# The first norm of token blocks 1 to 3 from a second layout of x

## The chip, the cores and the metric

The kernel runs on one core of a Trainium2 chip. The metric is device time of one execution in microseconds. Three runs of the kernel before took 2847.90, 2848.84 and 2848.22 us: median 2848.22. PE is TensorE, PEld its weight loads, DVE VectorE, ACT ScalarE, POOL GpSimd, and SP the engine whose queue starts every DMA here.

## The reference

One layer of a transformer trunk over 2048 tokens of 1024 features. Only the part at the start of it is touched:

```python
h = modulate(rms_norm(x, norm_g[i, 0]), sh_m, sc_m)   # h * (1 + scale) + shift
y = stick_breaking_mixer(h, sb_w_qkv[r], sb_w_o[r])   # 16 heads, first step h @ w_qkv
x = x + gt_m * rms_norm(y, norm_g[i, 1])
h = modulate(rms_norm(x, norm_g[i, 2]), sh_f, sc_f)
y = swiglu_ffn(h, ffn_w_in[i], ffn_w_out[i])
x = x + gt_f * rms_norm(y, norm_g[i, 3])
```

`rms_norm` divides each token's features by the root of their mean square and multiplies by a gain for each feature; `modulate` has a scale and a shift for each feature. So the first `h` is `x[t, d] * rstd[t] * g_eff[d] + shift[d]`: one number for a token, two for a feature.

## The kernel before, in words

The tokens are worked in four blocks of 512 (`BT`), the 1024 features in eight chunks of 128 (`KC`). Matrix products want `h` with features on the partitions, and they run as three float32r products (`mm3`, lines 169 to 171) of a high and a low part: high is the value rounded to float32r, low is the value less high. So a chunk of `h` is two 128x512 tiles, `hl[:, 0]` and `hl[:, 1]`, kept in pairs of chunks as `ht` tiles.

The projections make queries, keys and values for two heads at a time (a pair `p`) and one token block `b`. `STEPS` lists them: (0, 0), (1, 0), (0, 1), (0, 2), (0, 3), then the other pairs. A step (`project`) is a generator with three products of eight slices each: keys (t = 1), queries (t = 0), values (t = 2); a slice is one `mm3`, three 128x512 matmuls. The first 42 slices after step (0, 0) run by themselves; after that `project_to` mixes slices with the stages of attention (score, two sigmoids on ACT, a scan on DVE, a product on POOL, transposes on PE, their split into high and low on ACT and DVE, the weighing of values on PE). The four compute engines work in the order in which this code issues, each its own queue from front to back; the order of SP's transfers is the scheduler's.

The first norm of block `b` is issued from inside the step before it and its own first product:

- `x_load(b)`: four loads of 128 tokens, in tiles named `x`, from SP (line 306). Block 1 is loaded during step (0, 0); blocks 2 and 3 in the first slice of the keys product before.
- `x_square(b, i)`, slices 0 to 3 of the queries product: the sum of squares on ACT (line 160), its mean on DVE (162), the power -1/2 on POOL (164).
- `x_scale(b, i)`, slices 4 to 7: `xn` = x times the token's number, on DVE (315).
- `first_norm(b, k)`: chunks 0, 1 and 2 in slices 2, 4 and 6 of the values product, chunk k + 3 in slice k of the block's own keys product. `x_turn` transposes the chunk for four groups of 128 tokens on PE (324) into one PSUM tile `xT`; `modulate` makes `hf` = xT * gain + shift on ACT (334), the high part by a cast on DVE (340) and the low part by a subtraction (342), on DVE for blocks 1 and 2 and on POOL for block 3 (`HOW`). After two chunks SP stores the pair in `h_s` for the other heads (363).

The keys product of a step reads chunk k in slice k, so PE waits there for a chunk that isn't done. Block 0 goes another way (`full_high`, `low`), which the edit leaves.

Tiles come from pools by a tag with a fixed number of buffers: `v` 7 (the `x` tiles, values), `kt` 7 (`xn`, keys), `ht` 5, `tmp` 4 (`hf`). In PSUM, `tps` has two banks and `accps` three, which also hold the products' sums.

Of the kernel before, what the change touches and what calls it, by code (L numbers as in the profile page):

```python
# [9 lines left out]
F32 = mybir.dt.float32  # L10
# [64 lines left out]
HOW = ["aav", "avv", "avv", "avp"]  # L75


def f32(ap):
    return ap.bitcast(F32)
# [22 lines left out]
def hybrid_trunk_kernel(  # L102
    ctx: ExitStack,
    tc: tile.TileContext,
    x: bass.AP,
    c: bass.AP,
# [193 lines left out]
    x_tiles, x_norm, x_rstd = {}, {}, {}  # L300

    def x_load(b):
        for i in range(4):
            r0 = b * BT + i * P
            xt = att.tile([P, D], F32, name=f"x{b}_{i}", tag="v", bufs=BUFS["v"])
            nc.sync.dma_start(xt, x[r0 : r0 + P])
            x_tiles[b, i] = xt

    def x_square(b, i):
        xn = att.tile([P, D], F32, name=f"xn{b}_{i}", tag="kt", bufs=BUFS["kt"])  # L310
        x_norm[b, i] = xn
        x_rstd[b, i] = rms_scale(att, x_tiles[b, i], f"n0_{b}_{i}", junk=xn)
# [5 lines left out]

    def x_turn(b, k):

        pool, tag = (tps, "t") if b < 2 else (accps, "acc")
        pt = pool.tile([P, BT], F32, name=f"xT{b}_{k}", tag=tag)
        for i in range(4):
            nc.tensor.transpose(
                pt[:, i * P : (i + 1) * P], x_norm[b, i][:, k * P : (k + 1) * P], ident
            )
        return pt

    def modulate(hl, pt, which, k, name, how="aap"):

        full = att.tile([P, BT], F32, name=name, tag="tmp", bufs=BUFS["tmp"])
        gain, add = g_eff[:, which, k : k + 1], shift[:, which, k : k + 1]
        if how[0] == "a":
            nc.scalar.activation(full, pt, AF.Identity, bias=add, scale=gain)
        else:
            nc.vector.tensor_scalar(full, pt, gain, add, op0=ALU.mult, op1=ALU.add)
        if how[1] == "a":
            nc.scalar.copy(hl[:, 0], full)
        else:
            nc.vector.tensor_copy(hl[:, 0], full)  # L340
        eng = nc.gpsimd if how[2] == "p" else nc.vector
        eng.tensor_tensor(hl[:, 1], full, f32(hl[:, 0]), op=ALU.subtract)
# [11 lines left out]
    def first_norm(b, k):  # L354
# [6 lines left out]
        modulate(norm_h[b][k], x_turn(b, k), 0, k, f"hf{b}_{k}", HOW[b])  # L361
# [23 lines left out]
    def project(at):  # L385
# [10 lines left out]
        def product(t):  # L396
# [8 lines left out]
            for k in range(KC):  # L405
# [11 lines left out]
                if t == 0 and nb:  # L417
                    (x_square if k < 4 else x_scale)(nb, k % 4)
# [1187 lines left out]
```

## Time and profile before

| | us |
|---|---|
| median of three runs | 2848.22 |
| profiled execution | 2849.01 |
| its span, first to last instruction | 2846.9 |
| PE busy | 2797.7 |
| PE weight loads busy | 2333.6 |
| DVE busy | 2031.8 |
| ACT busy | 1629.6 |
| POOL busy | 1278.3 |

The granted clock of TensorE is 1.0 throughout. A row of the timeline has the start in us from the span's start, the duration, the engine, the line of the kernel, the operation, the tiles written and read, the shapes and the count; in brackets stands the idle time of the engine before it and what ended it. Matmuls are pipelined: each lasts longer than the time to the start of the next, so PE's pace is read from starts. A group's row has the count, then the busy time in us and the mean in ns, then the idle time before. All the first norm lies before 150 us.

### The profile page before, as it was taken

How to read it: one execution, taken by the hardware profiler on the slowest of the kernel's cores; microseconds unless marked ns; L12 is line 12 of the kernel's file. 1: busy time of each engine (PE TensorE's matmuls, PEld its weight loads, DVE VectorE, ACT ScalarE, POOL GpSimd, SP SyncE). 2: the span in 40 equal slices, each digit the busy share in tenths (PEclk: the TensorE clock that was granted, in tenths of full speed). 3: DMA queues.
4: the chain of work that ended last, by engine and by line, in shares of the span. 5: the costliest groups of instructions: out<-in, count | busy, mean ns of one | idle time of the engine just before them, and what ended most of it. 6: DMA issues, size and time to landing. Idle time of an engine off the chain costs nothing.

```text
span 2846.9 us, 41792 instructions
## 1 busy us (share of the span) xinstructions
PE 2797.7 (98%) x13848; PEld 2333.6 (82%) x13848; DVE 2031.8 (71%) x2825; ACT 1629.6 (57%) x3263; POOL 1278.3 (45%) x2032
## 2 busy tenths in 40 slices
PE   7999999999999999999999999999999999999998
PEld 6788888888888888887888888888788888888887
DVE  6788898888888888888866766555775665133477
ACT  4787877788787877777645533333433333322343
POOL 1475666666576655656410122221222222544454
PEclk9999999999999999999999999999999999999999
DMA  8765546656665635546289645334463335545565
GB/s 323 276 210 168 189 153 229 211 173 231 189 208 192 207 119 179 196 132 231 88 300 310 205 137 152 122 97 162 130 176 109 112 107 163 191 142 155 180 215 193
DMA packets 239368, 516.84 MB, mean 182 GB/s; under 512 B 22320, under 2 KB 110384, under 8 KB 221488
## 3 DMA queue, kind: packets, MB, share of 16 engines
q1 hardware_dynamic: 239152, 514.18, 55.7%
q8 instruction: 109, 1.79, 0.3%
q14 instruction: 107, 0.88, 0.1%
HBM read 346.85 MB, written 118.49 MB: 163 GB/s over the span
## 4 chain that ended last, share of the span: by engine, by line
PE 88%; DVE 5%; issue 2%; ACT 2%; DMA 1%; POOL 1%; SPq 0%; DVEq 0%; POOLq 0%; ACTq 0%
PE s L169 9%; PE s L171 9%; PE s L170 9%; PE z L528 8%; PE o L607 8%; PE t L579 8%; PE pj L169 6%; PE pj L170 6%; PE pj L171 6%; PE o L171 5%; PE o L169 5%; PE o L170 5%; PE y L171 1%; PE y L169 1%; PE y L170 1%
## 5 line engine op out<-in xcount | busy, mean ns | idle before, releaser
L569 POOL TENSOR_TENSOR a<-a,w 128x512 f32<-128x512 f32 (+3 forms) x640 | 620.0, 969 | 218.0 <-DVE w L562 127.1
L562 DVE TENSOR_TENSOR_SCAN w<-z,c,begin 128x512 f32<-128x512 f32 x384 | 489.4, 1279 | 82.0 <-ACT z L547 61.4
L169 PE MATMUL s<-r,l 128*128 128x512 f32 x1232 | 481.5, 391 | 4.3 <-DVE p L1369 3.9
L171 PE MATMUL s<-r,l 128*128 128x512 f32 x1232 | 479.5, 389 | 0.0
L170 PE MATMUL s<-r,l 128*128 128x512 f32 x1232 | 479.3, 389 | 0.0
L545 ACT ACTIVATE a<-z 128x512 f32<-128x512 f32 (+3 forms) x640 | 346.8, 542 | 167.4 <-PE z L528 137.1
L607 PE MATMUL o<-aT,v 128*128 128x512 f32 (+3 forms) x1280 | 384.2, 381 | 0.1
L595 DVE TENSOR_TENSOR aT<-t,aT 128x512 fp32r<-128x512 f32 (+3 forms) x640 | 358.9, 595 | 22.6 <-ACT aT L589 21.9
L528 PE MATMUL z<-kt,qt 128*128 128x512 f32 (+3 forms) x1280 | 363.1, 365 | 0.0
L589 ACT CAST aT<-t 128x512 fp32r<-128x512 f32 (+3 forms) x640 | 314.0, 533 | 73.8 <-PE t L579 63.6
L547 ACT ACTIVATE z<-z 128x512 f32<-128x512 f32 (+3 forms) x640 | 345.3, 539 | 0.0
L1377 POOL TENSOR_TENSOR one<-p,p 128x512 f32<-128x512 f32 x44 | 71.2, 1618 | 577.4 <-issue 320.3
L169 PE MATMUL pj<-ht,w 128*128 128x512 f32 x768 | 309.8, 403 | 6.3 <-issue 1.4
L170 PE MATMUL pj<-ht,w 128*128 128x512 f32 x768 | 302.2, 393 | 1.3 <-DVE ht L715 0.7
L579 PE MATMUL t<-begin,a 128*128 128x128 f32 x2176 | 294.8, 273 | 8.5 <-DVE aT L595 7.2
L579 PEld LDWEIGHTS t<-begin,a 128*128 128x128 f32 x2176 | 255.1, 140 | 58.1 <-DVE aT L595 11.0
L171 PE MATMUL pj<-ht,w 128*128 128x512 f32 x768 | 302.0, 393 | 0.0
L169 PEld LDWEIGHTS s<-r,l 128*128 128x128 f32 x1232 | 231.2, 188 | 54.5 <-ACT l L1230 2.9
L170 PEld LDWEIGHTS s<-r,l 128*128 128x128 f32 x1232 | 231.3, 188 | 48.5 <-issue 0.5
L171 PEld LDWEIGHTS s<-r,l 128*128 128x128 f32 x1232 | 231.2, 188 | 47.9
L557 DVE TENSOR_TENSOR_SCAN w<-z,begin 128x128 f32<-128x128 f32 (+3 forms) x256 | 208.7, 818 | 74.8 <-ACT z L547 63.3
L528 PEld LDWEIGHTS z<-kt,qt 128*128 128x128 f32 x1280 | 230.2, 188 | 37.4 <-DVE w L557 0.2
(160 smaller groups left out, 4866.5 us busy)
## 6 DMA issues: line engine op xcount, KB each, us to landing
ht<-h_s SPq DMA_DIRECT2D x108, 1024.0 KB, 8.0
wi<-in_win SPq DMA_DIRECT2D x86, 512.0 KB, 4.0
qt<-qn SPq DMA_DIRECT2D x124, 256.0 KB, 4.8
ol_qt<-act_s SPq DMA_DIRECT2D x56, 512.0 KB, 3.7
act_s<-S SPq DMA_DIRECT2D x66, 256.0 KB, 4.1
br<-in_wout SPq DMA_DIRECT2D x66, 256.0 KB, 3.6
h_s<-ht SPq DMA_DIRECT2D x16, 1024.0 KB, 7.9
o_s<-os SPq DMA_DIRECT2D x128, 128.0 KB, 2.7
```

The source lines that it names most:

```text
L169: nc.tensor.matmul(acc, lhs[0], rhs[0], start=first, stop=False, **kw)
L170: nc.tensor.matmul(acc, lhs[0], rhs[1], start=False, stop=False, **kw)
L171: nc.tensor.matmul(acc, lhs[1], rhs[0], start=False, stop=last, **kw)
L528: nc.tensor.matmul(z[:, :n], q[:, e, part, r * P : (r + 1) * P], k[:, e, :n], start=part == 0, stop=part == 1,)
L545: nc.scalar.activation(a[:, :n], z[:, :n], AF.Sigmoid, scale=QK_SCALE)
L547: nc.scalar.activation(z[:, :n], z[:, :n], AF.Sigmoid, scale=-QK_SCALE)
L562: nc.vector.tensor_tensor_scan(rest[:, rev], left[:, rev], begin[:, :BT][:, rev], initial=carries[r], op0=ALU.mult, op1=ALU.bypass,)
L569: nc.gpsimd.tensor_tensor(a[:, :n], a[:, :n], rest[:, 1 : n + 1], op=ALU.mult)
L579: nc.tensor.transpose(pt[:, rb * P : (rb + 1) * P], weighed[i, rb][:, j * P : (j + 1) * P], ident)
L589: nc.scalar.copy(hl[:, 0, t0:], pt[:, t0:])
L595: nc.vector.tensor_tensor(hl[:, 1, t0:], pt[:, t0:], f32(hl[:, 0, t0:]), op=ALU.subtract)
L607: nc.tensor.matmul(acc[:, t0:], lhs, hl[:, part, t0:], start=sc == qb and j == 0 and part == 0, stop=sc == 0 and j == 3 and part == 1,)
```

## The change

The host also lays out `x` of blocks 1 to 3 with features on the partitions, as a second input `xt`. For these blocks `x_load` loads both layouts: the `x` tiles as before, and four `xc` tiles of two chunks each (128 partitions, 2 x 512 tokens, 0.5 MB) in `kt` buffers. The squares are taken from `x` as before, now with the result written over `x`. `x_scale` is gone for these blocks. In its place:

- `x_spread(b)`, slice 5 of the queries product: on POOL, the first 128 columns of each `x` tile become the token's number in every column.
- `x_share(b)`, slice 0 of the values product: four transposes on PE turn these into one PSUM tile that has the 512 tokens' numbers as a row, the same on every partition; ACT copies it to the free half of the last `x` tile (`x_row`).
- `modulate`: DVE multiplies the chunk by gain and row in place (one operation), ACT adds the shift and writes the high part, DVE adds the shift and subtracts the high part (one operation), for all three blocks. `x_turn`, `x_norm`, `hf` and POOL's subtractions are no longer used for them.

Block 0 keeps its transposes. The places of `first_norm` in the steps are the same.

```diff
+    xt: bass.AP,
...
     def x_load(b):
         for i in range(4):
             r0 = b * BT + i * P
-            xt = att.tile([P, D], F32, name=f"x{b}_{i}", tag="v", bufs=BUFS["v"])
-            nc.sync.dma_start(xt, x[r0 : r0 + P])
-            x_tiles[b, i] = xt
+            tok = att.tile([P, D], F32, name=f"x{b}_{i}", tag="v", bufs=BUFS["v"])
+            nc.sync.dma_start(tok, x[r0 : r0 + P])
+            x_tiles[b, i] = tok
+        if b == 0:
+            return
+        for m in range(KC // 2):
+            cols = att.tile([P, 2, BT], F32, name=f"xc{b}_{m}", tag="kt", bufs=BUFS["kt"])
+            nc.sync.dma_start(cols, xt[b - 1, :, 2 * m : 2 * m + 2])
+            x_cols[b, 2 * m], x_cols[b, 2 * m + 1] = cols[:, 0], cols[:, 1]

     def x_square(b, i):
+        if b > 0:
+            tok = x_tiles[b, i]
+            x_rstd[b, i] = rms_scale(att, tok, f"n0_{b}_{i}", junk=tok)
+            return
...
+    def x_spread(b):
+        for i in range(4):
+            nc.gpsimd.tensor_scalar(
+                x_tiles[b, i][:, :P], ones, x_rstd.pop((b, i)), None, op0=ALU.mult
+            )
+
+    def x_share(b):
+        pool, tag = (tps, "t") if b < 2 else (accps, "acc")
+        pt = pool.tile([P, BT], F32, name=f"xr{b}", tag=tag)
+        for i in range(4):
+            tok = x_tiles.pop((b, i))
+            nc.tensor.transpose(pt[:, i * P : (i + 1) * P], tok[:, :P], ident)
+        x_row[b] = tok[:, BT:]
+        nc.scalar.copy(x_row[b], pt)
...
-    def modulate(hl, pt, which, k, name, how="aap"):
-
-        full = att.tile([P, BT], F32, name=name, tag="tmp", bufs=BUFS["tmp"])
-        gain, add = g_eff[:, which, k : k + 1], shift[:, which, k : k + 1]
-        if how[0] == "a":
-            nc.scalar.activation(full, pt, AF.Identity, bias=add, scale=gain)
-        else:
-            nc.vector.tensor_scalar(full, pt, gain, add, op0=ALU.mult, op1=ALU.add)
-        if how[1] == "a":
-            nc.scalar.copy(hl[:, 0], full)
-        else:
-            nc.vector.tensor_copy(hl[:, 0], full)
-        eng = nc.gpsimd if how[2] == "p" else nc.vector
-        eng.tensor_tensor(hl[:, 1], full, f32(hl[:, 0]), op=ALU.subtract)
+    def modulate(hl, b, k):
+
+        full = x_cols.pop((b, k))
+        add = shift[:, 0, k : k + 1]
+        nc.vector.scalar_tensor_tensor(
+            full, full, g_eff[:, 0, k : k + 1], x_row[b], op0=ALU.mult, op1=ALU.mult
+        )
+        nc.scalar.activation(hl[:, 0], full, AF.Identity, bias=add)
+        nc.vector.scalar_tensor_tensor(
+            hl[:, 1], full, add, f32(hl[:, 0]), op0=ALU.add, op1=ALU.subtract
+        )
...
-        modulate(norm_h[b][k], x_turn(b, k), 0, k, f"hf{b}_{k}", HOW[b])
+        modulate(norm_h[b][k], b, k)
...
-                if t == 0 and nb:
-                    (x_square if k < 4 else x_scale)(nb, k % 4)
+                if t == 0 and nb and k < 4:
+                    x_square(nb, k)
+                if t == 0 and nb and k == 5:
+                    x_spread(nb)
+                if t == 2 and nb and k == 0:
+                    x_share(nb)
...
+        "xt": get("x")[0].reshape(NB, BT, KC, P).transpose(0, 3, 2, 1)[1:],
```

More of the change, by code (lines that the diff above doesn't have):

```diff
@@ L73 @@
 LAST_HELD = 30
-HOW = ["aav", "avv", "avv", "avp"]
 def f32(ap):
@@ L297, in late_modulation @@
             yield
-    x_tiles, x_norm, x_rstd = {}, {}, {}
+    x_tiles, x_norm, x_rstd, x_cols, x_row = {}, {}, {}, {}, {}
     def x_load(b):
@@ L317, in x_scale @@
         )
+    def x_spread(b):
[11 more added lines that the diff above has]
+        nc.scalar.copy(x_row[b], pt)
     def x_turn(b, k):
-        pool, tag = (tps, "t") if b < 2 else (accps, "acc")
-        pt = pool.tile([P, BT], F32, name=f"xT{b}_{k}", tag=tag)
+        pt = tps.tile([P, BT], F32, name=f"xT{b}_{k}", tag="t")
         for i in range(4):
```

## The prediction

> **What bounds the kernel now.** I read the page's busy line and chain first, then the busy time by stretch, then each engine's timeline from 50 to 150 us, where the edited norm runs.
>
> ```profile
> PE 2797.7 (98%) x13848; PEld 2333.6 (82%) x13848; DVE 2031.8 (71%) x2825; ACT 1629.6 (57%) x3263; POOL 1278.3 (45%) x2032
> PE 88%; DVE 5%; issue 2%; ACT 2%; DMA 1%; POOL 1%; SPq 0%; DVEq 0%; POOLq 0%; ACTq 0%
> ```
>
> TensorE carries the whole: busy 98% of the span, 88% of the chain that ended last. The stretches of the edit look different (columns: stretch, its length, then busy us of PE, PEld, DVE, ACT and POOL with counts, the granted clock, DMA share, GB/s):
>
> ```profile
> 65.20:78.60 13.40, 13.36 (x75) 11.21 (x76) 10.04 (x18) 7.31 (x10) 0.00 (x0) 1.00 0.91 346
> 84.00:105.50 21.50, 19.57 (x105) 15.16 (x105) 17.80 (x30) 13.44 (x28) 5.18 (x13) 1.00 1.02 359
> 105.50:149.00 43.50, 40.25 (x224) 32.35 (x223) 37.45 (x55) 35.35 (x76) 31.50 (x55) 1.00 0.60 207
> 149.00:300.00 151.00, 150.90 (x835) 128.86 (x835) 126.40 (x164) 120.83 (x255) 97.60 (x206) 1.00 0.58 183
> ```
>
> The first three hold most of the norm of blocks 1, 2 and 3. DVE is busy 75, 83 and 86% of them, and in the second and third PE has holes of 2 and 3 us. From 149 us on PE has none: whatever is lost before is not won back there, and whatever is won stays won.
>
> **The change, part by part.** *Transposes.* Matmuls overlap, so what a group of four transposes costs is read from starts.
>
> ```profile
> 74.75 0.39 PE L171 MATMUL pj<-ht,w 128*128 128x512 f32 x1
> 74.98 0.60 PE L324 MATMUL xT<-begin,xn 128*128 128x128 f32 x4
> ...
> 75.64 0.39 PE L170 MATMUL pj<-ht,w 128*128 128x512 f32 x1
> ...
> 78.38 0.39 PE L171 MATMUL pj<-ht,w 128*128 128x512 f32 x1
> 78.61 0.39 PE L169 MATMUL pj<-ht,w 128*128 128x512 f32 x1
> ```
>
> Projection matmuls start 0.23 us apart (78.38, 78.61). From 74.75 to 75.64 lie two of them (the L171 shown and an L169) and four transposes: 0.89 - 0.46 = 0.43 us a group. Twenty-four groups go and three come: 21 x 0.43 = 9.0 us less work on PE, the most that PE can give directly.
>
> *Vector work.* Prices, from the groups by shape between 20 and 340 us (count | busy us, mean ns of one | idle before):
>
> ```profile
> L651 DVE SCALAR_TENSOR_TENSOR asum<-ac,c_act,asum 128x512 f32<-128x512 f32 x18 | 13.5, 750 | 0.4
> L315 DVE TENSOR_SCALAR xn<-x,n_rstd 128x1024 f32<-128x1024 f32 x12 | 8.8, 780 | 0.0
> L340 DVE CAST ht<-hf 128x512 fp32r<-128x512 f32 x24 | 14.1, 589 | 5.4 <-ACT hf L334 5.3
> L342 DVE TENSOR_TENSOR ht<-hf,ht 128x512 fp32r<-128x512 f32 x16 | 11.9, 746 | 0.6
> L342 POOL TENSOR_TENSOR ht<-hf,ht 128x512 fp32r<-128x512 f32 x8 | 10.3, 1289 | 2.8 <-DVE ht L340 2.8
> L334 ACT ACTIVATE hf<-xT,shift,g_eff 128x512 f32<-128x512 f32 x24 | 18.7, 779 | 16.3 <-PE xT L324 14.7 <-ACT z L547 1.0 <-ACT hf L334 0.6
> L710 ACT CAST ht<-hf 128x512 fp32r<-128x512 f32 x8 | 5.0, 620 | 0.3
> L470 ACT COPY vT<-pj 128x512 f32<-128x512 f32 x8 | 4.8, 595 | 2.0 <-PE pj L171 1.5 <-ACT z L547 0.4
> L569 POOL TENSOR_TENSOR a<-a,w 128x128 f32<-128x128 f32 x14 | 5.8, 416 | 8.2 <-DVE w L557 6.0 <-issue 2.0
> L568 POOL COPY c<-w 128x1 f32<-128x1 f32 x67 | 13.0, 193 | 46.6 <-DVE w L557 20.4 <-DVE w L562 16.7 <-ACT z L547 4.0
> ```
>
> DVE loses 12 scalings (L315, 12 x 0.78 = 9.4 us), 24 casts (14.1) and 16 subtractions (11.9), 35.4 us in all, and gains 48 two-tensor operations at 0.75, 36.0. By busy time that is even, and POOL loses 10.3. What changes is the order. Before, ACT made `hf` from PSUM ahead of DVE, and DVE cast and subtracted without a pause between. After, each chunk of 128 features goes DVE (gain and row), ACT (bias, high part), DVE (low part). DVE works its queue in order, and the two DVE operations of a chunk stand side by side in it: the low part waits there for ACT, and the next chunk's multiplication, whose data is ready, waits behind it.
>
> ```profile
> 45.02 0.16 DVE L679 SCALAR_TENSOR_TENSOR g_eff<-sc,gc 128x2 f32<-128x2 f32 x1
> 45.28 0.78 ACT L706 ACTIVATE hf<-xT,shift,g_eff 128x512 f32<-128x512 f32 x1 [4.61 <-DVE g_eff L679]
> 65.61 0.78 ACT L334 ACTIVATE hf<-xT,shift,g_eff 128x512 f32<-128x512 f32 x1 [1.98 <-PE xT L324]
> 66.42 0.43 DVE L340 CAST ht<-hf 128x512 fp32r<-128x512 f32 x1 [0.64 <-ACT hf L334]
> ```
>
> From DVE to ACT takes 0.10 (45.18 to 45.28), from ACT to DVE 0.03 (66.39 to 66.42). An Identity from SBUF with a bias alone is not in the trace. Its bounds: the plain cast from SBUF, 0.62, and the Identity with bias and gain from PSUM, 0.78. Bias and gain add 0.18 to the copy's 0.595; I put half of that on the cast and take 0.71. A chunk then takes 0.75 + 0.10 + 0.71 + 0.03 + 0.75 = 2.3 us. The ends are 2.06 (0.69 for each DVE operation, as the subtraction at 104.11 below took, 0.03 for both hand-overs, 0.62 for ACT) and 2.4 (0.78). [...]
>
> *Block 1.* The squares are unchanged and lead to the last power on POOL.
>
> ```profile
> 59.57 0.55 POOL L164 TENSOR_TENSOR n_rstd<-n_ms,mhalf 128x1 f32<-128x1 f32 x1 [41.66 <-DVE n_ms L162]
> 62.68 1.22 POOL L164 TENSOR_TENSOR n_rstd<-n_ms,mhalf 128x1 f32<-128x1 f32 x1 [0.49 <-DVE n_ms L162]
> 62.84 0.39 PE L169 MATMUL pj<-ht,w 128*128 128x512 f32 x1
> 65.24 0.33 PE L324 MATMUL xT<-begin,xn 128*128 128x128 f32 x1 [0.33 <-DVE xn L315]
> ```
>
> The last power starts at 62.68. It took 1.22 while DVE scaled beside it; without that I take the first one's 0.55, to 63.23. Then POOL makes four spreads of 128x128, each between a 128x1 copy (0.19) and a two-input product of that size (0.42): 0.3, to 64.45. PE comes to the row's transposes at 62.84 and stands there to about 64.6. The copy of the row on ACT starts 0.37 after the last of them, as `hf` did (65.24 to 65.61), takes 0.6 and ends at 65.5. Eight chunks: 65.56 + 8 x 2.3 = 84.0. The slice of the next step's first product that needs the last chunk ends two matmuls later, 84.5, where before it ended at 78.61: +5.9. In this stretch PE has no attention yet to put in between.
>
> *Block 2.* The chain starts again behind the next product and squares. Attention now stands between its chunks on DVE.
>
> ```profile
> 79.46 1.06 ACT L160 ACTIVATE xn<-x 128x1024 f32<-128x1024 f32 x1
> 91.93 0.42 DVE L557 TENSOR_TENSOR_SCAN w<-z,begin 128x128 f32<-128x128 f32 x1
> 93.99 0.68 DVE L557 TENSOR_TENSOR_SCAN w<-z,begin 128x256 f32<-128x256 f32 x1
> 95.25 0.96 DVE L557 TENSOR_TENSOR_SCAN w<-z,begin 128x384 f32<-128x384 f32 x1 [0.57 <-ACT z L547]
> 96.12 0.67 DVE L481 TENSOR_TENSOR v<-vt,v 128x512 fp32r<-128x512 f32 x1
> 98.17 1.22 DVE L557 TENSOR_TENSOR_SCAN w<-z,begin 128x512 f32<-128x512 f32 x1
> 104.11 0.69 DVE L342 TENSOR_TENSOR ht<-hf,ht 128x512 fp32r<-128x512 f32 x1
> 106.28 0.39 PE L169 MATMUL pj<-ht,w 128*128 128x512 f32 x1
> ```
>
> The first square starts 0.85 after the product (78.61 to 79.46), so at 85.3. Four squares end at 89.6, the mean and power at 90.4, the spreads at 91.6, the row is there at 92.7. Then 8 x 2.3 = 18.4, the five operations shown with the 128-wide scan a second time, 4.4, and 0.8 for ACT's sigmoids between them (bounds 0 and 1.5): the last chunk is done at 116.3, for 104.80 before. PE's first product of block 2 ends 0.5 later, 116.8, for 106.28: +10.5 up to here, the saved transposes included.
>
> *Block 3* runs inside attention.
>
> ```profile
> 105.50:149.00 43.50, 6.98 (x8) 6.24 (x8) 10.31 (x8) 1.00 0.60 207
> ```
>
> That is the part of `hf` in the third stretch (DVE, ACT, POOL). DVE's 37.45 us there lose 7.0 of casts and 4 x 0.78 = 3.1 of scalings; 27.4 stay, and eight chunks add 18.4 in which DVE works or stands: 45.8. If the 6 us in which DVE was idle all fill up, the stretch grows by 2; if none does, by 8. PE and POOL lose work here and ACT keeps 8 us of idle time, so a part fills: +4.
>
> *Transfers.* Twelve loads of 0.5 MB come.
>
> ```profile
> x<-in_x SPq DMA_DIRECT2D x12, 512.0 KB, 9.2
> ```
>
> They have the size of the `x` loads, which land after 9.2 us, and stand right behind them in SP's queue; the chain of block 2 needs its first one some 15 us after its issue, since the loads go out early in the slowed product. I cost them at nothing. If that cover is gone, 4.2 MB of blocks 2 and 3 at 359 GB/s are 11.7 us, and the `h_s` stores and `kt` and `qt` copies behind them are late too. SP also waits for block 0's last transposes before the last load of block 1, with the third weights of step (1, 0) behind it; those are used two products later. The row holds a `v` buffer until its block's last chunk; loads of the next block take the others.
>
> **Sum.** +10.5 + 4 = +14.5. The profiled execution took 2849.0 (span 2846.9), 0.8 above the median 2848.2: 2863.5 less 0.8, about 2862.5.
>
> **Rivals.** *A, faster: TensorE is the bound and gets its 9 us.* For it: 98% busy, 88% of the chain. It needs DVE to run chunk after chunk without a pause: block 1 breaks even at (78.1 - 65.56)/8 = 1.57 us a chunk, and two DVE operations alone are 1.5. Against it: the order on DVE. It gives 2848.2 - 9.0 = 2839. [...]
> *B, no difference:* block 3's attention fills all of DVE's new waits (-4), a chunk takes 2.06 (-3.8), spreads 0.2 (-0.8): 2853.9. Against it: DVE is 86% busy there already.
> *C, slower still, by transfers:* DMA stands at shares of 0.91 and 1.02 in the first two stretches; the 11.7 us all on the path give 2874. Against it: the loads' lead.
>
> **How the numbers follow.** Forecast 0.70, A 0.12, B 0.08, C 0.10. The forecast's own range goes from 2856 (2.06 a chunk, +2 in block 3) to 2869 (2.4, +8, spreads of 0.42). Up to C and down to B it is 2853 to 2874, which leaves out A and the tails. Below 0.2%, 5.7 us, a measurement hardly tells from no change: faster 0.12, same 0.08, slower 0.80.
>
> **What will show it.** Right: the low parts (new L361) idle DVE some 0.8 us each, waiting for ACT's Identity (new L360), in blocks 1 and 2; PE waits for `ht`, no longer for `xn`; the first product of block 1 ends near 84.5 us, of block 2 near 117; the stretch after that is some 4 us longer. Wrong: chunks closer than 1.6 us, or PE without holes there (A); ACT, DVE or PE waiting for `x`, `xc` or `wr` transfers (C); block 3 as long as before (B); a row copy much later than 65.5, which would mean that the spreads are mispriced.

## The result, and the profile after

The kernel after takes 2877.56 us (median of 4 runs, 2876.00 to 2880.63), beside 2848.53 for the kernel before (4 runs, 2847.90 to 2849.41). The ratio is 1.0103, 95% interval 1.0086 to 1.0121: slower by 29 us, where the forecast had 14.3 and its range ended at 2874. The profiled execution took 2878.73, its span is 2876.6.

The page of after, busy line and chain:

```profile
PE 2810.0 (98%) x13764; PEld 2337.6 (81%) x13764; DVE 2033.4 (71%) x2821; ACT 1630.5 (57%) x3266; POOL 1280.6 (45%) x2036
PE 83%; DVE 6%; DMA 3%; issue 3%; ACT 3%; POOL 1%; SPq 1%; DVEq 0%; POOLq 0%; ACTq 0%
```

PE has 84 instructions fewer (the 21 groups of transposes) and is busy 12 us longer. DVE's busy time is the same to 2 us. To see where the 29.7 us of span lie, I cut both spans where ACT starts to copy the keys (`kn`) out of PSUM: at the end of the first product of steps (1, 0), (0, 1), (0, 2) and (0, 3). The stretches between are called block 1, 2 and 3 below. Busy time by stretch, before (columns as in the prediction):

```profile
25.00:57.60 32.60, 30.06 (x165) 24.39 (x164) 22.83 (x42) 13.31 (x20) 0.00 (x0) 1.00 0.77 274
57.60:78.80 21.20, 20.87 (x109) 17.07 (x108) 14.65 (x28) 12.65 (x20) 2.86 (x4) 1.00 0.94 348
78.80:106.50 27.70, 25.77 (x132) 20.25 (x132) 19.95 (x35) 17.84 (x36) 7.36 (x18) 1.00 1.02 365
106.50:150.10 43.60, 40.35 (x225) 32.48 (x224) 37.55 (x55) 36.26 (x79) 31.81 (x54) 1.00 0.60 207
150.10:2846.90 2696.80, 2668.14 (x13181) 2229.66 (x13180) 1922.54 (x2638) 1536.22 (x3093) 1231.61 (x1947) 1.00 0.55 175
```

The same view of after:

```profile
25.00:59.50 34.50, 33.34 (x166) 27.33 (x165) 22.93 (x42) 13.30 (x19) 0.00 (x0) 0.90 0.83 290
59.50:87.90 28.40, 24.00 (x81) 15.31 (x81) 14.65 (x24) 12.65 (x22) 4.54 (x8) 0.87 0.95 363
87.90:122.10 34.20, 28.64 (x104) 20.78 (x104) 19.82 (x31) 17.59 (x37) 10.57 (x22) 0.81 0.96 338
122.10:179.80 57.70, 44.21 (x201) 35.32 (x200) 40.77 (x58) 36.68 (x79) 26.31 (x51) 0.85 0.58 196
179.80:2876.60 2696.80, 2667.35 (x13177) 2229.11 (x13175) 1920.97 (x2638) 1536.92 (x3093) 1234.64 (x1946) 1.00 0.54 175
```

The last stretch is 2696.8 us in both: nothing is lost or won once the norm is over. The loss is 1.9 us ahead of block 1, 7.2 in block 1, 6.5 in block 2 and 14.1 in block 3. DVE and ACT are no busier in blocks 1 and 2 (14.65 and 14.65; 19.95 and 19.82 for DVE). So there it is time in which engines stand; in block 3 DVE also has 3.2 us more work (40.77 for 37.55). The groups of after between 20 and 340 us show where they stand (lines of after: 357 gain and row, 360 shift and high part, 361 low part, 330 spread, 342 copy of the row):

```profile
L357 DVE SCALAR_TENSOR_TENSOR xc<-xc,g_eff,x 128x512 f32<-128x512 f32 x24 | 19.2, 798 | 3.0 <-ACT x L342 3.0
L361 DVE SCALAR_TENSOR_TENSOR ht<-xc,shift,ht 128x512 fp32r<-128x512 f32 x24 | 18.2, 760 | 19.3 <-ACT ht L360 19.3
L360 ACT ACTIVATE ht<-xc,shift 128x512 fp32r<-128x512 f32 x24 | 17.3, 722 | 38.8 <-DVE xc L357 38.8
```

DVE stands 19.3 us for ACT's high parts, 0.8 for each of the 24, and ACT stands 38.8 us for DVE's products. The chain of block 1, from its timelines on POOL, ACT and DVE:

```profile
64.59 0.55 POOL L162 TENSOR_TENSOR n_rstd<-n_ms,mhalf 128x1 f32<-128x1 f32 x1 [0.49 <-DVE n_ms L160]
65.13 2.35 POOL L330 TENSOR_SCALAR x<-ones,n_rstd 128x128 f32<-128x128 f32 x4
67.90 0.59 ACT L342 COPY x<-xr 128x512 f32<-128x512 f32 x1 [2.37 <-PE xr L340]
70.06 0.75 DVE L361 SCALAR_TENSOR_TENSOR ht<-xc,shift,ht 128x512 fp32r<-128x512 f32 x1 [0.79 <-ACT ht L360]
72.27 0.75 DVE L361 SCALAR_TENSOR_TENSOR ht<-xc,shift,ht 128x512 fp32r<-128x512 f32 x1 [0.79 <-ACT ht L360]
85.83 0.75 DVE L361 SCALAR_TENSOR_TENSOR ht<-xc,shift,ht 128x512 fp32r<-128x512 f32 x1 [0.79 <-ACT ht L360]
```

A chunk takes 2.2 us (70.06 to 72.27). The four spreads take 2.35. And from the end of the last low part (86.58) to the copy of the keys (87.90) pass 1.3 us. The clock column has 0.90, 0.87, 0.81 and 0.85 where before it was 1.00. Finer stretches of after show that it is halved for some microseconds at a time:

```profile
76.00:80.60 4.60, 2.66 (x9) 1.11 (x8) 3.02 (x5) 1.44 (x2) 0.00 (x0) 1.00 0.69 265
80.60:90.80 10.20, 9.81 (x22) 5.78 (x21) 5.21 (x10) 5.54 (x10) 0.57 (x1) 0.50 1.00 363
...
111.30:121.60 10.30, 9.08 (x22) 6.02 (x23) 7.19 (x11) 5.00 (x11) 2.48 (x7) 0.50 0.99 355
```

### The profile page after: what moved, and what is told of

Same layout as the page of the kernel before. It is cut to its first block, busy times and chain, and to the rows that moved or that the text cites. A ratio compares the mean times of both kernels' runs of the same rounds, so it can differ in the third digit from the quotient of the medians.

```text
span 2876.6 us, 41664 instructions
## 1 busy us (share of the span) xinstructions
PE 2810.0 (98%) x13764; PEld 2337.6 (81%) x13764; DVE 2033.4 (71%) x2821; ACT 1630.5 (57%) x3266; POOL 1280.6 (45%) x2036
## 4 chain that ended last, share of the span: by engine, by line
PE 83%; DVE 6%; DMA 3%; issue 3%; ACT 3%; POOL 1%; SPq 1%; DVEq 0%; POOLq 0%; ACTq 0%
PE s L167 9%; PE s L168 9%; PE s L169 9%; PE z L553 8%; PE o L632 8%; PE t L604 8%; PE pj L167 5%; PE pj L169 5%; PE pj L168 5%; PE o L169 4%; PE o L168 4%; PE o L167 4%; PE y L169 1%; PE y L167 1%; PE y L168 1%
## 5 line engine op out<-in xcount | busy, mean ns | idle before, releaser
L167 PE MATMUL pj<-ht,w 128*128 128x512 f32 x768 | 313.6, 408 | 10.9 <-ACT ht L360 5.3
L604 PEld LDWEIGHTS t<-begin,a 128*128 128x128 f32 x2176 | 256.7, 141 | 69.3 <-DVE aT L620 19.3
L168 PE MATMUL pj<-ht,w 128*128 128x512 f32 x768 | 307.0, 400 | 1.7 <-DVE ht L361 1.1
L169 PE MATMUL pj<-ht,w 128*128 128x512 f32 x768 | 305.8, 398 | 0.0
```

The source lines that it names most:

```text
L167: nc.tensor.matmul(acc, lhs[0], rhs[0], start=first, stop=False, **kw)
L168: nc.tensor.matmul(acc, lhs[0], rhs[1], start=False, stop=False, **kw)
L169: nc.tensor.matmul(acc, lhs[1], rhs[0], start=False, stop=last, **kw)
L604: nc.tensor.transpose(pt[:, rb * P : (rb + 1) * P], weighed[i, rb][:, j * P : (j + 1) * P], ident)
```

## The experiments

The theories: 1, the order on DVE, in which a low part stands for ACT and the next product behind it; 2, the halved clock as a loss of its own; 3, the new transfers; 4, POOL's spreads. Lengths of blocks 1, 2 and 3 are those of the windows from one copy of the keys to the next, in the profiled execution of each kernel; "start" is the first of these copies. A ratio is to runs of the kernel before taken beside that row's, whose medians lie between 2848.5 and 2851.0; so medians of two rows can differ by some 2 us for that alone.

| kernel | median us | ratio to before, 95% | start | block 1 | 2 | 3 |
|---|---|---|---|---|---|---|
| before | 2848.5 | | 57.6 | 21.2 | 27.7 | 43.6 |
| after | 2877.6 | 1.0103 (1.0086 to 1.0121) | 59.5 | 28.4 | 34.2 | 57.7 |
| product ahead | 2863.8 | 1.0047 (1.0032 to 1.0062) | 58.0 | 21.5 | 32.9 | 50.0 |
| no spreads | 2870.4 | 1.0070 (1.0055 to 1.0085) | 57.7 | 25.8 | 32.0 | 54.3 |
| both edits | 2858.3 | 1.0033 (1.0020 to 1.0046) | 57.7 | 19.2 | 34.1 | 48.2 |
| extra matmuls | 2877.7 | 1.0100 (1.0085 to 1.0115) | 60.9 | 27.9 | 34.6 | 57.9 |
| loads twice | 2882.8 | 1.0111 (1.0094 to 1.0128) | 63.0 | 28.6 | 33.6 | 59.9 |
| new in block 1 alone | 2857.9 | 1.0028 (1.0016 to 1.0040) | 60.7 | 28.4 | 27.2 | 43.5 |
| new in block 3 alone | 2864.0 | 1.0049 (1.0034 to 1.0064) | 61.1 | 21.2 | 29.4 | 56.6 |
| block 3, low part on POOL | 2876.7 | 1.0093 (1.0076 to 1.0109) | 57.8 | 28.4 | 33.8 | 60.5 |
| block 3 all on DVE | 2877.0 | 1.0081 (1.0065 to 1.0098) | 60.6 | 28.4 | 34.3 | 56.3 |
| block 3 product ahead | 2869.5 | 1.0071 (1.0055 to 1.0087) | 57.7 | 28.4 | 32.7 | 49.2 |
| both edits, blocks 1, 2 | 2854.7 | 1.0014 (1.0005 to 1.0023) | 60.8 | 19.2 | 34.5 | 43.6 |
| the same, block 2 loaded early | 2854.3 | 1.0009 (1.0000 to 1.0018) | 60.1 | 19.2 | 29.3 | 48.0 |
| the same, POOL helps | 2854.9 | 1.0010 (1.0000 to 1.0019) | 57.8 | 21.0 | 28.1 | 47.8 |
| blocks 2 and 3 loaded early | 2850.4 | 1.0001 (0.9992 to 1.0010) | 57.5 | 19.2 | 29.9 | 43.6 |
| both edits, block 1, early loads | 2846.2 | 0.9987 (0.9977 to 0.9996) | 60.7 | 19.2 | 27.1 | 43.5 |
| again, on another chip | 2849.1 | 0.9995 (0.9986 to 1.0004) | 60.2 | 19.2 | 26.7 | 43.6 |
| early loads alone | 2851.0 | 0.9999 (0.9990 to 1.0008) | 60.7 | 21.2 | 26.3 | 43.6 |

The start scatters between 57.5 and 61.1 from one profiled execution to the next, with no relation to the edits (more on that below; 63.0 in one case has its own cause). So a difference of 3 us between medians of few runs says little, and the lengths of the blocks say more.

### The next chunk's product ahead of the low part

```diff
+        if k == 0:
+            gained(0)                       # the product with gain and row
         nc.scalar.activation(hl[:, 0], full, AF.Identity, bias=add)
+        if k + 1 < KC:
+            gained(k + 1)
         nc.vector.scalar_tensor_tensor(hl[:, 1], full, add, ...)
```

> One change to the kernel after: DVE makes the gain and row of chunk k+1 before the low part of chunk k, so that it no longer stands behind ACT's Identity. Theory 1 (the order on DVE behind ACT is the main loss, as forecast, and the lost clock follows from the holes that it makes): the low parts idle DVE by less than 0.1 us instead of 0.79, a chunk of blocks 1 and 2 takes 1.5 to 1.6 us instead of 2.2, 8 x 0.7 = 5 to 6 us come back in each of these two blocks and a few in block 3: 2860 to 2866 us, against 2877.6. Theory 2 (the halved clock is a loss of its own, which the chunks' order does not cause): the order brings back less than 5 us and most of the 44 us at half clock stay: 2870 to 2876. Theory 3 (the new transfers): no change, 2875 to 2880.

2863.8, so 13.8 us come back by the medians and 15.9 by the three blocks: theory 1. Between 20 and 340 us the groups of this kernel have the same operations with the standing gone (368 is the low part, 365 the high part):

```profile
L368 DVE SCALAR_TENSOR_TENSOR ht<-xc,shift,ht 128x512 fp32r<-128x512 f32 x24 | 20.5, 854 | 1.0 <-ACT ht L365 0.5
L365 ACT ACTIVATE ht<-xc,shift 128x512 fp32r<-128x512 f32 x24 | 17.1, 722 | 13.8 <-DVE xc L357 10.9 <-DMA wr<-in_wqkv 2.9
```

DVE's wait falls from 19.3 to 1.0 us, ACT's for DVE from 38.8 to 10.9. A chunk of block 1 takes 1.33 us, less than the forecast's 1.5 for its two DVE operations alone: these start 0.66 us apart (the product between the two rows below starts at 69.21), though each is listed with 0.75.

```profile
68.54 0.75 DVE L368 SCALAR_TENSOR_TENSOR ht<-xc,shift,ht 128x512 fp32r<-128x512 f32 x1
69.87 0.75 DVE L368 SCALAR_TENSOR_TENSOR ht<-xc,shift,ht 128x512 fp32r<-128x512 f32 x1
```

Block 1 gets back 6.9 of its 7.2 us, and its clock is at 1.00 again throughout; block 3 gets back 7.7 of 14.1. Block 2 gets only 1.3 of the 5 to 6 expected. Its row starts to be copied 10.5 us after the copy of the keys, for 8.4 in after: ACT stands 1.2 us for the first `x` tile, of which more comes below, and 3.3 for the row's transposes.

### POOL's spreads left out

```diff
-                if t == 0 and nb and k == 5:
-                    x_spread(nb)
...
-            nc.tensor.transpose(pt[:, i * P : (i + 1) * P], tok[:, :P], ident)
+            nc.tensor.transpose(pt[:, i * P : (i + 1) * P],
+                                x_rstd.pop((b, i)).to_broadcast((P, P)), ident)
```

> The kernel after without POOL's four spreads per block: the transposes of the row read each token's scale directly, repeated over 128 columns. Theory 4 (the spread, 0.587 us each instead of the 0.3 that the forecast took, is a main part of the overrun): 4 x 0.587 = 2.35 us come off in front of the chunks of blocks 1 and 2, and part of it in block 3: 5 to 7 us, 2871 to 2873. Theory 1 (order on DVE): the same direction, as the chunks then start earlier, but the rest of the loss stays. Theory 3 (transfers): no change, 2875 to 2880. If the transposes of a repeated column take longer than those of a full tile, part of the gain goes.

2870.4, 7.2 less, a little more than theory 4 had: it holds. The transposes take the repeated column as it is, at 0.276 us a time, and the three blocks are 2.6, 2.2 and 3.4 us shorter than in after. Against before they still lack 4.6, 4.3 and 10.7, which the spreads don't explain.

### Both edits

> Both edits that have won time, together: the next chunk's multiplication ahead of the low part on DVE, and the row straight from the scales without POOL's spreads. Singly they gave 13.8 and 7.2 us. Theory 1 with 4 as separate terms (period of a chunk, start of the chain): they add up, 2855 to 2858; block 1's stretch then takes some 20 us, block 2's about 30, and what is left over 2848 is block 3. Rival: in blocks 1 and 2 TensorE becomes the limit, and a part is counted twice: 2859 to 2862. Below 2848 only if block 3's loss goes as well.

2858.3, between the two forecasts. By the blocks the gains don't add up: 15.9 and 8.2 us singly, 18.8 together. Block 1 is now 2.0 us shorter than before the change, so PE's saving can be won there (81 matmuls for 109: seven groups, 3.0 us at 0.43). Block 2 is 6.4 longer, for a new reason. The waits of ACT in block 2 of this kernel:

```profile
ACT ht L367 <- DVE xc L359: 5.3, 6, 1.7
ACT x L158 <- DMA x<-in_x: 4.9, 1, 4.9
```

The squares of block 2 start 4.9 us late, since the first `x` tile isn't there: the loads stand in SP's queue behind two stores, and DMA has a share of 1.01 in both stretches. The 4.9 us are about what is missing from the sum. With block 1 9.2 us shorter than in after, the forecast's rival C comes in.

### Extra matmuls that keep PE at work

```diff
+            nc.tensor.matmul(acc[:32], idle_weights, rhs, start=False, stop=False)
```

Weights are zero; four of these stand before each slice but the first of block 1's keys product, two in blocks 2 and 3, and four before each of attention's turns while the sum is open.

> The kernel after, with extra matmuls with weights of zero into a sum that is open anyway, before slices of the first product of blocks 1 to 3 and before attention's turns while that sum is open: TensorE keeps working where it would stand and wait, and the results stay the same. It changes no order on DVE, ACT or POOL. Theory 1 (order on DVE): the chunk period stays at 2.2 us, the first products of blocks 1 and 2 end little earlier, and only what is counted at half clock while work is waiting comes back: 2868 to 2876 us. Theory 2 (the halved clock is a loss of its own): the clock stays near 1.0 after 45 us and some 10 us or more come back: 2858 to 2868. Theory 3 (transfers): no change. If the extra matmuls themselves stand in the way, slower than 2880.

2877.7: no change, where theories 1 and 2 expected a gain; no change is also what theory 3 had, on which the next run bears. The clock is 1.00 in blocks 1 and 2 of this kernel and 0.88 in block 3:

```profile
60.90:88.80 27.90, 25.69 (x109) 17.10 (x108) 14.61 (x24) 12.63 (x22) 4.53 (x8) 1.00 0.95 363
88.80:123.40 34.60, 28.59 (x126) 19.50 (x125) 19.82 (x31) 17.61 (x36) 10.83 (x22) 1.00 0.98 343
123.40:181.30 57.90, 49.67 (x227) 37.65 (x227) 40.92 (x58) 36.81 (x80) 26.15 (x50) 0.88 0.57 194
```

With the full clock block 1 is 0.5 us shorter and block 2 is 0.4 longer: the half clock is no loss of 10 us. In block 2 the run doesn't separate it cleanly, because ten of the extra matmuls stand in PE's queue between the last two slices, in groups of four, four and two (at 118.99, 120.27 and 122.07). At 0.23 us from start to start they take 2.3 us. In after, the half clock stretches that same place:

```profile
120.89 0.63 PE L167 MATMUL pj<-ht,w 128*128 128x512 f32 x1
121.31 0.52 PE L168 MATMUL pj<-ht,w 128*128 128x512 f32 x1
121.67 0.40 PE L169 MATMUL pj<-ht,w 128*128 128x512 f32 x1
121.90 0.39 PE L167 MATMUL pj<-ht,w 128*128 128x512 f32 x1
```

Starts lie 0.42 us apart before 121.6 and 0.23 after it. So the half clock's own cost in blocks 1 and 2 is an estimated 1 to 2 us: 0.5 in block 1 by this run, and in block 2 at most half of the 2.4 us between last chunk and copy. In block 3 it wasn't isolated: a mean clock of 0.85 over 57.7 us is 17 us at half clock, so its cost there has an estimated upper bound of half of that, 8.7 us.

### Every new load twice

```diff
-            nc.sync.dma_start(cols, xt[b - 1, :, 2 * m : 2 * m + 2])
+            for _ in range(2):
+                nc.sync.dma_start(cols, xt[b - 1, :, 2 * m : 2 * m + 2])
```

> The kernel after with each of the twelve new loads issued twice: 6.3 MB more, some 18 us of transfers at the 350 GB/s of the first stretches. Theory 3 (the transfers of x with features on the partitions, and what stands behind them in SP's queue, cost time): the loss of these loads doubles, 5 us or more slower than after, above 2883. Theories 1, 2 and 4: the loads have cover, 2875 to 2881. A larger share of half clock before 45 us would speak for the loads as the cause of the 1.9 us by which the kernel after is late there.

2882.8, 5 us more by the medians, between the two forecasts, which looks like theory 3. But the place is another: ahead of block 1, where ACT's copy of the keys of step (1, 0) now waits for a transfer of the one before (waits of this kernel, 50 to 64 us):

```profile
ACT kn L457 <- DMA kt<-kn: 5.2, 1, 5.2
```

`xc` loads stand in SP's queue among the `kt` copies, and the two buffers of `kn` come free late; hence the start at 63.0. Besides, the last `xc` load goes out at 55.49 here, behind the first `kt` copy (51.31), with the other three `kt` copies behind it (55.86); in after it goes out at 45.57, and the four `kt` copies follow together from 52.86. So the edit does more than double the transfers. Blocks 1 and 2 have 28.6 and 33.6 us, together no longer than in after, with all the added transfers; block 3 has 2.2 more. In after that copy waited for PE alone, and between 20 and 180 us no engine waits for an `x` or `xc` transfer: the single loads have cover.

### One block alone

```diff
+NEW = {1}                      # {3} in the second run
...
-        modulate(norm_h[b][k], b, k)
+        if b in NEW:
+            modulate(norm_h[b][k], b, k)
+        else:
+            modulate_turned(norm_h[b][k], x_turn(b, k), 0, k, f"hf{b}_{k}", HOW[b])
```

`modulate_turned` is `modulate` of before; loads, squares, scalings and spreads follow the same test.

> The new form for block 1 alone; blocks 2 and 3 as in the kernel before. In the kernel after, the stretch of block 1 is 7.2 us longer than before (start of the kn copy on ACT, from step (1, 0) to step (0, 1)). Theory 1 (order on DVE and spread in that block): these 7 us stay to the end, as TensorE has no holes later: 2854 to 2858 us. Rival: block 2 or 3 of the old form makes up for a part, as their attention is only shifted: 2849 to 2853. If more than 2860 comes out, block 1 also costs something in the blocks behind it.

2857.9 with a start 3.1 us late in the profiled execution; its blocks are 28.4, 27.2 and 43.5. Block 1's 7.2 us stay, and the old form behind it loses nothing.

> The new form for block 3 alone; blocks 1 and 2 as in the kernel before. The forecast put +4 us on block 3 (2852); in the trace of after its stretch is 14.1 us longer than before. Theory 5a (the loss is block 3's own: attention's operations on DVE queue behind low parts that wait for ACT, and TensorE waits for attention): 2860 to 2864. Theory 5b (block 3 mostly pays for the late and half clocked start that blocks 1 and 2 leave to it): 2851 to 2856.

2864.0, with 56.6 us in block 3: 13.0 of the 14.1 us are block 3's own. 5b falls. Block 2, in the old form, takes 29.4 us here for 27.7: the clock is 0.94 there, and PE is busy 27.33 us with the same 132 matmuls that took 25.77. Some 3.5 us at half clock thus go with 1.7 us lost in the old form as well. So the step of the forecast that said +4 has to be found inside block 3.

### Block 3: three ways to take the low part from behind ACT

First the low part on POOL, for block 3:

```diff
+        if b == 3:
+            nc.scalar.activation(full, full, AF.Identity, bias=add)
+            nc.gpsimd.tensor_tensor(hl[:, 1], full, f32(hl[:, 0]), op=ALU.subtract)
+            return
```

> The kernel after, in block 3 alone with the low part off DVE: ACT makes the high part and then the full value in two Identity operations (8 x 0.72 = 5.8 us more on ACT), POOL subtracts (8 x 1.29 = 10.3 us, as it did before the change). Theory 5a (DVE's work and its waits in block 3 hold up attention, and through it TensorE): block 3's 14 us fall to 4 to 8, 2867 to 2872. Rival (ACT is the limit of that stretch, or POOL's 1.29 us take the low part's place in the chain): 2875 or slower.

Then all three operations on DVE:

```diff
-        nc.scalar.activation(hl[:, 0], full, AF.Identity, bias=add)
+        if b == 3:
+            nc.vector.tensor_scalar(hl[:, 0], full, add, None, op0=ALU.add)
+        else:
+            nc.scalar.activation(hl[:, 0], full, AF.Identity, bias=add)
```

> The kernel after, with block 3's high part made by DVE as well (it adds the shift and casts), so that a chunk of block 3 is three operations on DVE one after another and ACT has no part in it: DVE gets some 8 x 0.5 = 4 us more work, ACT 8 x 0.72 less. Theory 6 (block 3 loses its time by the meetings of the two queues: DVE stands 6.3 us for ACT, ACT stands 15.6 us for DVE with attention's sigmoids behind it): both waits go, and block 3's stretch falls from 14.1 us over the time before to 5 to 9, in spite of the added work: 2868 to 2873. Rival (DVE's work is block 3's limit): 2880 or slower.

And the order of the first experiment in block 3 alone:

```diff
+        if k == 0 or b < 3:
+            gained(k)
         nc.scalar.activation(hl[:, 0], full, AF.Identity, bias=add)
+        if k + 1 < KC and b == 3:
+            gained(k + 1)
```

> The kernel after, with the next chunk's multiplication ahead of the low part in block 3 alone. No engine gets more or less work; only the standing goes. Theory 6 (DVE's 6.3 us behind ACT and ACT's 15.6 us behind DVE are block 3's loss): both fall below 3 us, block 3's stretch goes from 14.1 us over the time before to 5 to 7, blocks 1 and 2 stay: 2868 to 2872. Rival (the plain work on DVE, 3.3 us more than before, and late starts make the loss): 2875 or slower.

The first two missed: 60.5 and 56.3 us in block 3. The third came out as theory 6 had it: 49.2. Groups of DVE and ACT in block 3, first of after:

```profile
L361 DVE SCALAR_TENSOR_TENSOR ht<-xc,shift,ht 128x512 fp32r<-128x512 f32 x8 | 6.2, 776 | 6.3 <-ACT ht L360 6.3
L360 ACT ACTIVATE ht<-xc,shift 128x512 fp32r<-128x512 f32 x8 | 5.8, 723 | 15.6 <-DVE xc L357 15.6
```

With the low part on POOL:

```profile
L360 ACT ACTIVATE ht<-xc,shift 128x512 fp32r<-128x512 f32 x8 | 5.8, 720 | 14.0 <-DVE xc L357 14.0
120.00:180.50 60.50, 45.92 (x201) 36.18 (x201) 34.84 (x50) 42.11 (x87) 33.97 (x59) 0.83 0.54 189
```

With all on DVE (361 the high part, 364 the low part):

```profile
L361 DVE TENSOR_SCALAR ht<-xc,shift 128x512 fp32r<-128x512 f32 x8 | 7.0, 878 | 0.3
L364 DVE SCALAR_TENSOR_TENSOR ht<-xc,shift,ht 128x512 fp32r<-128x512 f32 x8 | 6.0, 751 | 0.3
123.30:179.60 56.30, 43.76 (x197) 35.03 (x196) 46.71 (x65) 32.51 (x72) 25.01 (x50) 0.85 0.57 199
```

With the product ahead in block 3:

```profile
L368 DVE SCALAR_TENSOR_TENSOR ht<-xc,shift,ht 128x512 fp32r<-128x512 f32 x8 | 7.4, 924 | 0.1
L365 ACT ACTIVATE ht<-xc,shift 128x512 fp32r<-128x512 f32 x8 | 5.8, 721 | 3.9 <-DMA wr<-in_wqkv 2.9 <-DVE xc L357 1.0
118.80:168.00 49.20, 40.75 (x197) 32.13 (x196) 41.80 (x60) 36.78 (x81) 28.50 (x53) 0.93 0.60 210
```

In after DVE is taken for 40.77 + 6.3 = 47.1 us of block 3, working or standing. All on DVE it is 46.7 of work and 0.6 of standing: the wait has become work (the high part took 0.88 us a time, not the 0.5 expected), and the time stays. With POOL, DVE works only 34.8 us, but ACT gets 42.1 us of work and still stands 14.0 for DVE's products: the wait behind DVE was left in place, and ACT is taken for 56.1 of 60.5. Only the order takes the standing from both and adds nothing: 41.8 us of DVE, 8.5 us back. What PE waits for, in block 3 of before, after, and with the product ahead:

```profile
PE t L579 <- DVE aT L595: 1.0, 3, 0.5
```
```profile
PE t L604 <- DVE aT L620: 11.6, 6, 4.8
```
```profile
PE t L611 <- DVE aT L627: 6.5, 5, 3.0
```

PE stands at attention's transposes until DVE has made the low part of the transposed weights (`aT`). So the chain is: DVE late, then attention, then PE. That blocks 1 and 2 of this run are 28.4 and 32.7, nearly those of after, shows that the gain is block 3's. Of its 5.6 us over before the runs don't say how much is DVE's added work (41.80 against 37.55 us) and how much the half clock. Nor do they split the 8.5 us: the time at half clock falls with the order, from 17 to 7 us (0.93 over 49.2), so up to 5 us of the gain, an estimate as above, can have come back through the clock.

### Toward a faster kernel

Both edits with `NEW = {1, 2}`, block 3 as before the change:

> The next chunk's multiplication ahead, no spreads (the two edits together), and the new form in blocks 1 and 2 alone, block 3 as before. Milestones of the two edits together: block 1's stretch 2.0 us shorter than before the change, block 2's 6.4 longer, block 3's 4.6 longer. If block 3's loss is its own (theory 5a), it goes and 2852 to 2854 us are left. If the old form of block 3 suffers from what stands before it (5b), 2855 to 2859.

2854.7, between the two ranges; the block decides: block 3's loss goes with its new form (43.6). Then block 2's token loads ahead of the two stores, for which the row moves to a `tmp` buffer, so that the `x` tiles come free sooner:

```diff
                 if t == 2 and nb in NEW and k == 0:
                     x_share(nb)
+                    if nb == 1:
+                        x_early(2)       # the four loads of x; the xc loads stay
```

> The new form in blocks 1 and 2 with both edits, block 3 as before, and the four token loads of block 2 issued right behind the row of block 1 rather than behind two stores in SP's queue (in the run with both edits ACT stood 4.91 us for the first of them). Theory 7 (with shorter chunks the loads are the next to come late: the forecast's rival C in small): block 2's stretch falls by 4 to 5 us against the run without the early loads: 2847 to 2849. Rival (the DMA engines are full there, shares of 1.0, and the loads land no earlier): 2851 to 2854.

Block 2 is 5.2 us shorter, as theory 7 has it, but the median stays (2854.3, not 2847 to 2849): block 3 loses 4.4 us, since ACT now stands for the loads of block 3.

```profile
113.49 1.06 ACT L162 ACTIVATE xn<-x 128x1024 f32<-128x1024 f32 x1 [4.27 <-DMA x<-in_x]
```

A gain was handed on as a wait for the next transfer. With POOL making half of the products in block 1:

```diff
+            if b == 1 and j % 2:
+                nc.gpsimd.tensor_tensor(col, col, x_row[b], op=ALU.mult)
...
+        if b == 1 and k % 2:
+            nc.scalar.activation(hl[:, 0], full, AF.Identity, bias=add, scale=gain)
+            nc.scalar.activation(full, full, AF.Identity, bias=add, scale=gain)
```

> As the run with the early loads, and in block 1 POOL makes the product of the odd chunks with the row (128x512, 1.29 us by the group of before), ACT then makes high part and full value with gain and shift, and DVE only subtracts: DVE's work for two chunks falls from 3.0 to 2.25 us. Theory 1 (DVE sets the period in block 1): block 1 ends some 2 to 3 us earlier, 2844 to 2847, if the loads of block 2 follow. Rival (TensorE or the loads are the limit by then): no gain, 2847 to 2851.

2854.9, worse than both forecasts. Block 1 takes 21.0 us, longer by 1.8. POOL's four products took 1.6 us each for the 1.29 taken (POOL is busy 8.56 us in 8 operations there, for 2.19 in 4). DVE has four operations fewer (20 for 24) and is busy 14.75 us, not less than the 14.09 without POOL's help; at the pace without it the twenty would take an estimated 11.1 (14.09 less four products at 0.75). ACT is busy 15.78 us for 12.51. Without that, but with block 3's loads early too (`if nb < 3: x_early(nb + 1)`):

> As the run with the early loads of block 2, and block 3's four token loads behind the row of block 2 as well. In that run ACT stood 4.3 us for the first token tile of block 3, and block 3's stretch was 48.0 us against 43.6. Theory 7 (the loads are the next limit): block 3 falls back to 43.6 to 44.5: 2848 to 2851, level with the kernel before. Rival (the DMA engines are full, what is loaded earlier delays something else): 2852 to 2855.

Block 3 is back at 43.6, and the kernel level with the one before (1.0001). Its block 2 still takes 2.2 us more than the old form. Last, the new form in block 1 alone (`NEW = {1}`), with both sets of early loads; then these loads without it (`NEW = set()`), and the version with both again, on one chip:

> The new form in block 1 alone, with the multiplication ahead and no spreads, blocks 2 and 3 as before the change but with their token loads issued early. Block 1's stretch was 2.0 us shorter so than before the change; if blocks 2 and 3 take no longer than before, 2845 to 2848, by 2 us or less the fastest of all. Rival (block 1's gain is lost in block 2 by loads or by the old form's waits): 2848 to 2851.

> The kernel before (old form in all blocks), with the token loads of blocks 2 and 3 issued early, in the last product of the step before. By the milestones of the version with block 1 in the new form, block 1 gives 2.0 us and block 2 0.6 us. If the earlier loads give only the 0.6, this is 0 to 1 us faster than the kernel before; if they give most of the gain, 2 us or more.

> The version with block 1 in the new form (multiplication ahead, no spreads) and early token loads, again, beside the early loads alone: 2 to 4 us faster than the kernel before, and 1.5 to 2.5 us faster than the early loads alone if block 1's new form is what wins.

The version with both is at 0.9987 (0.9977 to 0.9996) on one chip and 0.9995 (0.9986 to 1.0004) on another; the early loads alone at 0.9999. The repeat was expected 2 to 4 us faster than before and is 1 us faster, with no change inside its interval. In the profiles block 1's new form takes 19.2 us against 21.2, and block 2 then 26.7 to 27.1 against 26.3. So block 1 is worth some 1.5 us, by these rows; in the medians that is shown on the one chip and lies within the scatter on the other.

## Why the prediction was wrong

The sign and the mechanism were right, the size wasn't: the forecast's four terms against the profile (the parts of +10.5 are 5.9 for block 1 and 4.6 for block 2).

| term | forecast | measured |
|---|---|---|
| ahead of block 1 | 0 | +1.9 |
| block 1 | +5.9 | +7.2 |
| block 2 | +4.6 | +6.5 |
| block 3 | +4, ends +2 and +8 | +14.1 |
| sum | +14.5 | +29.7 |

*A chunk at 2.3 us: right, a little high.* Measured 2.2 in block 1: 0.75, 0.72 for ACT, 0.75, and next to nothing for the hand-overs. The first experiment shows that it is this order that costs.

*The spreads at 0.3 each: wrong.* They took 0.587, above the two-input product of that size (0.416), which I had as the upper end. With the 1.9 us of the start taken off, the last power ended at 63.23, where the forecast had it; the spreads at 65.57 instead of 64.45; the row's copy at 66.58 instead of 65.5. That is 1.1 us in block 1, and the run without spreads got back 2 to 3 us in each block.

*"Two matmuls later" and "0.5 later": wrong.* From the last low part to the copy of the keys it took 1.3 us in block 1 and, from 119.67 to 122.10, 2.4 in block 2, at half clock, and in block 2 with attention's transposes between the last slices. The forecast never asked what the holes it put into PE would do to the clock, a term that it left out. In after the clock was 0.50 for 10.2 and 10.3 us (from 80.6 and from 111.3), and its means in blocks 1 and 2 were 0.87 and 0.81; with the extra matmuls both were 1.00. Ahead of the first of these stretches PE was busy 2.66 of 4.60 us (76.0 to 80.6), and its longest wait in block 1 was 0.9 us. What starts such a stretch, and what sets its length, is not shown.

*Block 3, "so a part fills: +4": the step that failed.* The first half of it stands. I had DVE working or standing 45.8 us, and it was 47.1. But I let part of DVE's idle time fill up, because "ACT keeps 8 us of idle time". DVE's other idle time did not shrink, it grew, from 5.2 us (43.6 less 37.55 busy, less 0.8 in front of the casts) to 10.6 (57.7 less 40.77, less 6.3). With the 8.7 us that DVE was taken for longer, that is the 14.1. Most of the growth stands in front of attention's scans and of `aT`, 2.8 us before and 7.2 after. DVE in block 3, before:

```profile
L562 DVE TENSOR_TENSOR_SCAN w<-z,c,begin 128x512 f32<-128x512 f32 x8 | 10.2, 1273 | 1.2 <-ACT z L547 1.2
L595 DVE TENSOR_TENSOR aT<-t,aT 128x512 fp32r<-128x512 f32 (+3 forms) x18 | 9.3, 531 | 0.3 <-ACT aT L589 0.2
L557 DVE TENSOR_TENSOR_SCAN w<-z,begin 128x512 f32<-128x512 f32 (+3 forms) x10 | 8.1, 812 | 1.3 <-ACT z L547 1.1
```

After:

```profile
L587 DVE TENSOR_TENSOR_SCAN w<-z,c,begin 128x512 f32<-128x512 f32 x8 | 10.2, 1281 | 1.6 <-ACT z L572 1.6
L620 DVE TENSOR_TENSOR aT<-t,aT 128x512 fp32r<-128x512 f32 (+3 forms) x17 | 8.7, 526 | 2.4 <-ACT aT L614 2.4
L582 DVE TENSOR_TENSOR_SCAN w<-z,begin 128x512 f32<-128x512 f32 (+3 forms) x10 | 8.2, 821 | 3.2 <-ACT z L572 3.1
```

ACT works its queue in order as well; its Identity stood 15.6 us for DVE's product, with attention's sigmoids and casts behind it. I counted the meeting once, as DVE's wait for ACT; it is a wait on both sides. The run with the product ahead shows what the order is worth: DVE taken for 41.9 us and 7.3 of other idle time, so 5.2 and 3.3 us back. It doesn't show that ACT's standing alone made the idle time grow. All on DVE, ACT has no part in the chunks, and yet scans and `aT` wait 5.5 us and the other idle time is 9.0. That the idle time could not be filled is shown. How its growth splits between ACT's queue, DVE's late work that comes back through PE and ACT, and the half clock stays open.

*The start: +1.9, not the change.* Five kernels with all the new loads start at 57.7 to 58.0. The early loads alone, whose norm has the old form, start at 60.7. Its first stretch has the same 165 matmuls as before and PE busy 35.25 us with them, not 30.06:

```profile
25.00:60.70 35.70, 35.25 (x165) 29.23 (x164) 22.87 (x42) 13.30 (x20) 0.00 (x0) 1.00 0.70 251
```

So the same matmuls took longer together; its clock column reads 1.00, and what slowed them is not shown. Two more late starts have the same column and PE busy as long: block 1 with early loads (60.7) 35.25 us, extra matmuls (60.9) 35.44. In after, which starts at 59.5, it is 33.34 us (166 matmuls), and there the clock is seen: it was 0.50 from 30.3 to 36.1 us, with projection matmuls 0.42 to 0.43 us apart (33.48, 33.91, 34.33) and 0.23 apart later (39.44, 39.67, 39.91). Before has 1.00 from 30.3 to 36.1, and 0.23 to 0.24 (33.29, 33.52, 33.76). What lets the full clock come early or late is not shown. About 2 of the 29 us can be this scatter.

*The rivals.* A fell as the forecast had it, since no chunk came under 2.2 us; with the product ahead and no spreads it holds for block 1, at -2.0 us. The break-even of 1.57 us a chunk was too kind, as it had the spreads too short: at 1.33, with the spreads, block 1 was still 0.3 us longer than before; it won only without them. B fell. C fell for the kernel after, and came true in small once the chain was shorter: 4.9 us in block 2, then 4.3 in block 3.

## What to carry to other kernels

When one step of a chain goes to another engine and back, look at what stands behind it in both queues: each side waits for the other (in after 19.3 us of DVE for ACT and 38.8 of ACT for DVE), and idle time in such a stretch can be waiting of the same chain, which more work did not fill here but lengthened (DVE's in block 3 from 5.2 to 10.6 us). Issue the next item's first operation ahead of the last one's end before judging such a form; that alone gave back half of this loss. And where a chain gets shorter, look next at the loads: twice here a gain was followed by a wait for a transfer that had been hidden (4.9 and 4.3 us).

## What the runs showed of the hardware

A POOL product of a 128x128 float32 tile with one number per partition took 0.587 us in block 1 of after (four in 2.35), more than the product of two such tiles in before (0.416). In after TensorE's clock was 0.50 for 10.2 us from 80.6 on though PE had been busy 2.66 of the 4.60 us before and had waited 0.9 us at the longest in block 1. Two of DVE's eight products in block 3 of after took 1.28 and 1.29 us (147.30, 166.53), each beside a 128x512 product of POOL (146.95, 166.17); the other six took 0.72 to 0.75. Where POOL's product started 0.23 us after DVE's (143.19, 173.77), POOL's took 1.45 us, otherwise 1.09 or 1.10 in that block. And a column repeated 128 times went through PE's transposes like a full tile, in 0.276 us a time where the transposes of `xT` in before have 0.278 (in the kernel without spreads, between 20 and 340 us):

```profile
L340 PE MATMUL xr<-begin,n_rstd 128*128 128x128 f32 x12 | 2.0, 276 | 0.0
```
